# Sparse attention: scaling the probabilities one turn ahead of their transposes

## The chip, the core and the metric

The kernel runs on one core of one Trainium2 chip. The core has a matrix engine (TensorE, PE in the profile; its weight loads are the row PEld), a vector engine (DVE), a scalar engine (ACT), a general engine (GpSimd, POOL) and an engine that issues transfers (SyncE, SP). All work on a shared on-chip memory, SBUF; the matrix engine writes its results into eight PSUM banks. The metric is the device time of one execution in microseconds; a lower one is better.

## The reference

One decoder layer on 512 tokens of width 1024 in float32: a half-step feed-forward network, a token mixer, a second half-step feed-forward network, each between RMS norms. The token mixer adds native sparse attention and dilated attention. The change lies in the sparse attention, which has 8 heads of width 64 on 2 key groups and three branches:

```python
g = jax.nn.sigmoid(gates)
return g[..., 0:1] * o_cmp + g[..., 1:2] * o_slc + g[..., 2:3] * o_win
```

Each branch is a softmax over biased scores times values. With 512 tokens the selected branch takes all of its 8 blocks of 64, and the window of 512 covers everything, so both the selected and the window branch are full causal attentions, with keys and values of their own. Dividing a row of probabilities by its sum and weighting the branch by its gate are one factor to a query row, gate over sum.

## The kernel before

All products with weights run as three matmuls on high and low parts (`mm3`, lines 128 to 132), the parts made by a cast on ACT (line 107) and a subtraction on DVE (line 108). `nsa` (line 1006) does the sparse attention. It first makes keys, values, gates and the inputs of the compressed branch, then runs a loop of turns over a list of 16 entries, `heads`: 4 query tiles times 2 halves times 2 branches (0 selected, 1 window). An entry is called a head here. With `LAG = 2` there are 18 turns; turn n scores head n and finishes head n-2. In the order of the program a turn holds:

- in every fourth turn, the query projection of the next tile, and `cmp_pair` (line 909), the compressed branch of two heads;
- `hb_probs` (line 961) for head n-2: `gated` (lines 905 to 907) makes four factors, gate over sum, by three small DVE instructions; the probabilities of four query tiles are multiplied by them in place, those of tile 3 (512 columns) on ACT (line 969), those of the other three (384, 128 and 256 columns) on POOL (line 971); then ten transposes on PE (line 980) bring them into three PSUM banks, tag T, of which there are two, and each bank is split into a high and a low part (lines 107 and 108);
- `hb_scores` (line 945) for head n: for three PSUM banks of tag S, matmuls for the scores (lines 724 and 725), then for each query tile a DVE instruction that adds the position bias and takes the extreme of a row (the min-add, line 730), and an exponential on ACT that also sums the row (line 731). The results lie in three of 11 SBUF slots, tag SP;
- `hb_values` (line 992) for head n-2: eight matmuls (line 995) of the transposed probabilities with the values into a bank of tag V, and after the window branch the compressed part and `fold` (line 998);
- in the first turns the compressed branch's hidden layer, and in every third turn a filler (`merge_unit`, line 1079), a projection for a later stage.

Every instruction belongs to one engine, and the engine runs its own in a fixed order. That order is made when the program is compiled: a planner that works with its own estimates of durations goes through the instructions, gives each engine those whose inputs are ready, and takes the one that stands earlier in the program where several are. A stretch of the program can be kept in written order; `nsa` does not do that. Semaphores then make each instruction wait for its inputs.

Of the kernel before, what the change touches and what calls it, by code (L numbers as in the profile page):

```python
# [60 lines left out]
class Layer:  # L61
# [896 lines left out]
                self.softmax_rows(pt[n][:, o:o + ncol], b[:, o:o + ncol], w[:, S - ncol:S], st[:, 0, t:t + 1], st[:, 1, t:t + 1])  # L958
        return st, pt

    def hb_probs(self, st, pt, gate):

        nc = self.nc
        self.gated(st[:, 1], NT, gate)
        for t in (3, 2, 0, 1):
            n, o = self.PLACE[t]
            pp = pt[n][:, o:o + (t + 1) * P]
            if t == NT - 1:
                nc.scalar.mul(pp, pp, st[:, 1, t:t + 1])
            else:  # L970
                nc.gpsimd.tensor_scalar(pp, pp, st[:, 1, t:t + 1], None, op0=OP.mult)  # L971
        out = {}
        for kbs in ((0,), (1, 3), (2,)):
            b = self.bank("T")
            ncols = 0
            for kk in kbs:
                _, o = self.TPLACE[kk]
                for t in range(kk, NT):
                    pn, po = self.PLACE[t]
                    nc.tensor.transpose(b[:, o + (t - kk) * P:o + (t - kk + 1) * P],  # L980
                                        pt[pn][:, po + kk * P:po + (kk + 1) * P], self.ident)
                    ncols += P
            hi, lo = self.slot("PT", F32R)[:, 0:ncols], self.slot("PT", F32R)[:, 0:ncols]
            self.split(hi, lo, b[:, 0:ncols])
            for kk in kbs:
                _, o = self.TPLACE[kk]
                c = slice(o, o + (NT - kk) * P)
                out[kk] = hi[:, c], lo[:, c]
        return out
# [16 lines left out]
    def nsa(self, fillers):  # L1006
        nc = self.nc
        ident = lambda v: v
        r = self.wcols([(C_KC, 256)])
        src = [r[:, :, 0:P], r[:, :, P:2 * P]]  # L1010
        r2 = self.wcols([(C_KS, P), (C_KW, P)])
        src2 = [r2[:, :, 0:P], r2[:, :, P:2 * P]]
        early = []
        for s, tag in zip(src + src2, "FFSV"):
            w = self.wslots(s, "SP") if tag == "V" else None
            early.append(self.proj_T(s, self.bank(tag), (0, 2 * P), w))
            if len(early) in (2, 3):
                self.pending.pop(0)()
        for n, (b, w) in enumerate(early):
            self.proj_T(None, b, (2 * P, S), w)  # L1020
        rows = [self.block_rows(b) for b, _ in early[:2]]
        kw = early[3][0]
        vw = self.v_weights()
        kparts = [self.k_parts(early[2][0], ident)]
        gs = [self.blocks(0, rows[0])]
        kparts.append(self.k_parts(kw, ident))
        gs.append(self.blocks(1, rows[1]))
        self.v_nsa(vw)
        early = self.hidden_early(0)
        self.oh, self.ol = [], []  # L1030
        heads = [(i, half, br) for i in range(4) for half in range(2) for br in range(2)]
        qs, cmps, ws, live = {}, {}, {}, {}
        probs = {}
        for n in range(len(heads) + LAG):
            if n < len(heads) and n % 4 == 0:
                i = n // 4
                b, _ = self.proj_T(self.wcols([(i * 64, 64), (256 + i * 64, 64)]))
                qs[i] = self.q_parts(b, ident)
                if i:
                    cmps[i] = self.cmp_pair(i, qs[i])  # L1040
            m = n - LAG
            if m >= 0:
                i, half, br = heads[m]
                probs[m] = self.hb_probs(*live.pop(m), self.gate[:, :, (i + 4 * half) * 3 + 1 + br])
            if n < len(heads):
                i, half, br = heads[n]
                h = i + 4 * half
                if br == 0:
                    ws[h] = self.slot("W")
                    nc.vector.tensor_scalar(ws[h], self.dm, -(2.0 ** -(h + 1)), None, op0=OP.mult)  # L1050
                kb, ka = kparts[br]
                live[n] = self.hb_scores(qs[i][half], ka[half], kb, half, ws[h])
            if m >= 0:
                i, half, br = heads[m]
                if br == 0:
                    out = self.bank("V")
                    if half == 0:
                        of = self.slot("of")
                self.hb_values(probs.pop(m), br, half, out, br == 0)
                if br == 1:  # L1060
                    nc.tensor.matmul(out, self.vcs[half], cmps[i], start=False, stop=True, skip_group_check=True)
                    self.fold(of, half, out[0:64], out[64:128])
                    if half == 1:
                        hi, lo = self.slot("x", F32R), self.slot("x", F32R)
                        self.split(hi, lo, of)
                        self.oh.append(hi)
                        self.ol.append(lo)
            if n < 2:
                self.hidden(n, gs[n], early)
                if n == 0:  # L1070
                    early = self.hidden_early(1)
                else:
                    hid = self.gelu()
            if n == 2:
                self.compressed(hid)
                cmps[0] = self.cmp_pair(0, qs[0])
            fillers()
# [465 lines left out]
```

## Time and profile before

| | us |
|---|---|
| median of 3 runs | 1134.19 |
| lowest and highest run | 1133.87, 1138.51 |
| the profiled execution | 1135.51 |
| its span, first to last instruction | 1133.7 |
| PE busy in the span | 1119.2 |
| DVE busy | 907.2 |
| ACT busy | 638.1 |
| POOL busy | 76.8 |

The times are of whole executions; the profile is of one execution, and its span leaves out what lies before the first and after the last instruction. A row of a profile that groups instructions has line, engine, operation, what is written and read, shapes and count, then the busy time and the mean duration in ns, then the idle time of that engine in front of them and what ended it. A row of the timeline has start, duration, engine, line and the same names, and in brackets the idle time in front. PE's busy time is modelled at its ends: consecutive matmuls overlap, so that a short wait need not show as idle time. The loop of turns lies between 398 and 533 us.

### The profile page before, as it was taken

Reading aid. Unit: us, or ns where it says so; the run is one execution under the profiler, and the core shown is the slowest. Engines: PE = TensorE matmul, PEld = TensorE weight load, DVE = VectorE, ACT = ScalarE, POOL = GpSimd, SP = SyncE. Lnnn points to the kernel's source line nnn. Section 1 sums busy time; section 2 is a strip of 40 time slices with the busy share of each in tenths; the row PEclk is TensorE's granted clock in tenths of the full one; section 3 lists DMA queues with packets and bytes.
Section 4 is the critical chain, followed back from the end, with each engine's and each line's share of the span. In section 5 each row is a group of like instructions: output and inputs, shape, how many; then the busy total and the mean of one; then the engine's idle time right before and its main releaser. Section 6 shows DMA issues by size and latency. Waiting matters only on the chain.

```text
span 1133.7 us, 18456 instructions
## 1 busy us (share of the span) xinstructions
PE 1119.2 (99%) x6921; PEld 1001.7 (88%) x6921; DVE 907.2 (80%) x1563; ACT 638.1 (56%) x1145; POOL 76.8 (7%) x112
## 2 busy tenths in 40 slices
PE   9999999999999999999999999999999999999997
PEld 7889999998888987778888998787989999998886
DVE  6989999879676889687665687986778888979774
ACT  5435555567563788677565634645445555557562
POOL 1000000000012033343000000000000000000000
PEclk9999999999999999999999999999999999999999
DMA  9996665588763542111476758683233424357862
GB/s 320 328 305 194 182 209 173 155 273 287 266 204 96 176 131 85 54 40 56 140 251 224 253 177 292 210 290 118 66 121 122 131 86 127 124 170 239 285 224 84
DMA packets 152908, 206.01 MB, mean 182 GB/s; under 512 B 19794, under 2 KB 97906, under 8 KB 152564
## 3 DMA queue, kind: packets, MB, share of 16 engines
q1 hardware_dynamic: 152816, 204.85, 55.7%
q8 instruction: 54, 0.88, 0.3%
q14 instruction: 34, 0.28, 0.1%
q10 hardware_dynamic: 4, 0.00, 0.0%
HBM read 165.45 MB, written 39.37 MB: 181 GB/s over the span
## 4 chain that ended last, share of the span: by engine, by line
PE 89%; DVE 5%; ACT 2%; issue 1%; DMA 1%; POOL 1%; SPq 0%; POOLq 0%; DVEq 0%; ACTq 0%
PE pb_F L132 11%; PE pb_F L130 11%; PE pb_F L131 11%; PE pb_S L132 8%; PE pb_S L131 8%; PE pb_S L130 8%; PE pb_T L130 6%; PE pb_T L132 6%; PE pb_T L131 6%; PE pb_V L131 3%; PE pb_V L130 3%; PE pb_V L132 3%; PE pb_V L995 2%; PE pb_T L980 1%; DVE SP_s L730 1%
## 5 line engine op out<-in xcount | busy, mean ns | idle before, releaser
L107 ACT CAST whi<-raw 128x1024 fp32r<-128x1024 f32 (+1 forms) x215 | 219.9, 1023 | 251.9 <-issue 68.2
L108 DVE TENSOR_TENSOR wlo<-raw,whi 128x1024 fp32r<-128x1024 f32 (+1 forms) x215 | 255.0, 1188 | 94.9 <-ACT whi L107 91.3
L130 PE MATMUL pb_F<-xh_t,whi 128*128 128x512 f32 (+1 forms) x392 | 142.7, 364 | 0.4 <-ACT whi L107 0.4
L132 PE MATMUL pb_F<-xh_t,wlo 128*128 128x512 f32 (+1 forms) x392 | 141.6, 361 | 0.5 <-DVE wlo L108 0.5
L131 PE MATMUL pb_F<-xl_t,whi 128*128 128x512 f32 (+1 forms) x392 | 141.8, 362 | 0.0
L107 ACT CAST whi<-tmp_t 128x1024 fp32r<-128x1024 f32 x51 | 53.5, 1048 | 60.9 <-PE pb_S L131 22.0
L132 PEld LDWEIGHTS pb_F<-xh_t,wlo 128*128 128x128 f32 x392 | 74.1, 189 | 10.8 <-DVE wlo L108 1.0
L130 PEld LDWEIGHTS pb_F<-xh_t,whi 128*128 128x128 f32 x392 | 74.1, 189 | 10.4 <-ACT whi L107 0.6
L131 PEld LDWEIGHTS pb_F<-xl_t,whi 128*128 128x128 f32 x392 | 74.2, 189 | 9.6
L108 DVE TENSOR_TENSOR wlo<-tmp_t,whi 128x1024 fp32r<-128x1024 f32 x51 | 62.4, 1223 | 25.2 <-ACT whi L107 23.9
L130 PE MATMUL pb_S<-xh_t,whi 128*128 128x256 f32 (+1 forms) x240 | 73.2, 305 | 0.0
L132 PE MATMUL pb_S<-xh_t,wlo 128*128 128x256 f32 (+1 forms) x240 | 73.0, 304 | 0.0
L131 PE MATMUL pb_S<-xl_t,whi 128*128 128x256 f32 (+1 forms) x240 | 73.0, 304 | 0.0
L130 PE MATMUL pb_T<-xh_t,whi 128*128 128x256 f32 (+1 forms) x184 | 54.5, 296 | 0.0
L132 PE MATMUL pb_T<-xh_t,wlo 128*128 128x256 f32 (+1 forms) x184 | 54.3, 295 | 0.0
L131 PE MATMUL pb_T<-xl_t,whi 128*128 128x256 f32 (+1 forms) x184 | 54.3, 295 | 0.0
L152 POOL TENSOR_TENSOR rs_t<-rs_t,mhalf_t 128x1 f32<-128x1 f32 x24 | 17.5, 727 | 542.7 <-DVE rs_t L148 542.7
L971 POOL TENSOR_SCALAR SP_s<-SP_s,st_t 128x384 f32<-128x384 f32 (+2 forms) x48 | 45.8, 970 | 107.1 <-DVE st_t L907 77.3
L131 PEld LDWEIGHTS pb_S<-xl_t,whi 128*128 128x128 f32 x240 | 45.9, 191 | 1.9
L130 PEld LDWEIGHTS pb_S<-xh_t,whi 128*128 128x128 f32 x240 | 45.9, 191 | 1.9
L132 PEld LDWEIGHTS pb_S<-xh_t,wlo 128*128 128x128 f32 x240 | 45.9, 191 | 1.9
L108 DVE TENSOR_TENSOR PT_s<-pb_T,PT_s 128x512 fp32r<-128x512 f32 (+1 forms) x72 | 39.2, 559 | 6.3 <-ACT PT_s L107 5.6
(822 smaller groups left out, 3363.8 us busy)
## 6 DMA issues: line engine op xcount, KB each, us to landing
raw<-in_ffn_w_up_dram SPq DMA_DIRECT2D x36, 512.0 KB, 5.3
raw<-in_w_in_dram SPq DMA_DIRECT2D x18, 1024.0 KB, 5.7
raw<-in_ffn_w_gate_dram SPq DMA_DIRECT2D x35, 512.0 KB, 4.9
raw<-in_ffn_w_down_dram SPq DMA_DIRECT2D x14, 1024.0 KB, 5.7
raw<-tdram SPq DMA_DIRECT2D x14, 1024.0 KB, 5.2
NN_s<-in_ffn_w_down_dram SPq DMA_DIRECT2D x22, 512.0 KB, 5.0
tdram<-NN_s SPq DMA_DIRECT2D x22, 512.0 KB, 3.9
raw<-in_ffn_w_down_dram SPq DMA_DIRECT2D x6, 768.0 KB, 5.8
```

The lines of the kernel that those rows point to most:

```text
L107: self.last_cast = self.nc.scalar.copy(dsthi, src).ins
L108: self.last_rest = self.nc.vector.tensor_sub(dstlo, src, dsthi.bitcast(F32)).ins
L130: mm(out, lhi, rhi, start=start, stop=False, skip_group_check=skip)
L131: mm(out, lhi, rlo, start=False, stop=False, skip_group_check=skip)
L132: mm(out, llo, rhi, start=False, stop=stop, skip_group_check=skip)
L152: nc.gpsimd.tensor_tensor(out=r, in0=v, in1=self.mhalf, op=OP.pow)
L730: nc.vector.tensor_tensor_reduce(p, s, w, -1.0, FLOOR, OP.add, OP.min, st_m)
L971: nc.gpsimd.tensor_scalar(pp, pp, st[:, 1, t:t + 1], None, op0=OP.mult)
L980: nc.tensor.transpose(b[:, o + (t - kk) * P:o + (t - kk + 1) * P], pt[pn][:, po + kk * P:po + (kk + 1) * P], self.ident)
L995: self.nc.tensor.matmul(out[:, kk * P:S], v, pp, start=first and kk == 0 and pi == 0, stop=False, skip_group_check=True)
```

## The change

`hb_probs` is cut in two. `hb_scale` holds `gated` and the four multiplies, `hb_probs` the transposes and splits. In turn n, the transposes of head n-2 are emitted first, then the scaling of head n-1, then the scores of head n. So the scaling of a head stands one turn earlier in the program than its transposes, behind the transposes of the head before it and ahead of the scores of the head after it. The number and kind of instructions stays the same, and so does what each of them reads and writes.

```diff
-    def hb_probs(self, st, pt, gate):
+    def hb_scale(self, st, pt, gate):
 
         nc = self.nc
         self.gated(st[:, 1], NT, gate)
...
             else:
                 nc.gpsimd.tensor_scalar(pp, pp, st[:, 1, t:t + 1], None, op0=OP.mult)
+
+    def hb_probs(self, pt):
+
+        nc = self.nc
         out = {}
         for kbs in ((0,), (1, 3), (2,)):
             b = self.bank("T")
...
             m = n - LAG
             if m >= 0:
-                i, half, br = heads[m]
-                probs[m] = self.hb_probs(*live.pop(m), self.gate[:, :, (i + 4 * half) * 3 + 1 + br])
+                probs[m] = self.hb_probs(live.pop(m)[1])
+            if 0 <= n - 1 < len(heads):
+                i, half, br = heads[n - 1]
+                self.hb_scale(*live[n - 1], self.gate[:, :, (i + 4 * half) * 3 + 1 + br])
             if n < len(heads):
                 i, half, br = heads[n]
                 h = i + 4 * half
```

## The prediction, made before the changed kernel ran

> **What bounds the kernel now.** I read the page first, then the busy time of the attention stage by stretches, then the rows of the instructions that the change moves, then who waits for them.
>
> ```profile
> span 1133.7 us, 18456 instructions
> PE 1119.2 (99%) x6921; PEld 1001.7 (88%) x6921; DVE 907.2 (80%) x1563; ACT 638.1 (56%) x1145; POOL 76.8 (7%) x112
> ...
> PE 89%; DVE 5%; ACT 2%; issue 1%; DMA 1%; POOL 1%; SPq 0%; POOLq 0%; DVEq 0%; ACTq 0%
> ```
>
> The page says that TensorE (PE) works in 99% of the span and carries 89% of the chain that ended last; 1133.7 - 1119.2 = 14.5 us are all the idle time that it shows. A change gains only what it takes from PE's work or from PE's waits. The change touches neither a matmul nor a transpose, so only waits are left, and only those of the sparse attention, which lies between 398 and 535 us:
>
> ```profile
> core 0: us, PE busy (x) PEld busy (x) DVE busy (x) ACT busy (x) POOL busy (x), PEclk, DMA share, GB/s
> 400.00:430.00 30.00, 29.28 (x173) 24.55 (x172) 25.48 (x78) 23.78 (x61) 8.76 (x9) 1.00 0.39 98
> 430.00:460.00 30.00, 29.53 (x173) 23.71 (x172) 27.70 (x86) 25.59 (x62) 14.68 (x15) 1.00 0.25 79
> ...
> sum 135.00, PE 133.46 PEld 108.01 DVE 112.15 ACT 103.22 POOL 48.41; mean PE 26.69 PEld 21.60 DVE 22.43 ACT 20.64 POOL 9.68
> ```
>
> Of these 135 us PE is idle in 1.54, DVE in 22.85, ACT in 31.78, POOL in 86.6; the clock is full. Matmul ends are modelled and overlap, so PE's small waits hide inside its busy time; they show better at the weight loads (PEld), each of which must have its operand:
>
> ```profile
> PEld pb_V L995 <- ACT PT_s L107: 4.0, 13, 0.7
> PEld pb_T L980 <- DVE PT_s L108: 1.8, 6, 0.4
> PEld pb_S L724 <- DVE st_t L730: 1.6, 6, 0.6
> PEld pb_V L995 <- DVE PT_s L108: 1.4, 6, 0.3
> ```
>
> These are the largest such waits between 395 and 540 us (us in total, times, longest). The transposes (L980) wait for the split that empties their PSUM bank, the value matmuls (L995) for the split of the transposed probabilities. No row names the scaling, POOL's L971 or ACT's L969, as what a load on PE waited for.
>
> **The scaling is already far ahead.** In the program the scaling of head m stands in turn m+2 right in front of its transposes. The rows of the trace show another order. First POOL's own rows, then the first transposes of the same heads on PE; heads are counted in order, three POOL instructions and ten transposes to a head (0, 3, 5 and 6 in one row, 7, 14, 15):
>
> ```profile
> 409.18 2.99 POOL L971 TENSOR_SCALAR SP_s<-SP_s,st_t 128x384 f32<-128x384 f32 x3 [50.19 <-DVE st_t L907]
> ...
> 432.53 3.54 POOL L971 TENSOR_SCALAR SP_s<-SP_s,st_t 128x384 f32<-128x384 f32 x3 [8.91 <-DVE st_t L907]
> ...
> 451.20 5.78 POOL L971 TENSOR_SCALAR SP_s<-SP_s,st_t 128x384 f32<-128x384 f32 x6 [6.62 <-DVE st_t L907]
> 457.74 2.73 POOL L971 TENSOR_SCALAR SP_s<-SP_s,st_t 128x384 f32<-128x384 f32 x3 [0.76 <-PE pb_T L980]
> ...
> 517.76 2.73 POOL L971 TENSOR_SCALAR SP_s<-SP_s,st_t 128x384 f32<-128x384 f32 x3 [1.07 <-DVE st_t L907]
> 522.28 2.73 POOL L971 TENSOR_SCALAR SP_s<-SP_s,st_t 128x384 f32<-128x384 f32 x3 [1.79 <-DVE st_t L907]
> ```
>
> ```profile
> 413.90 1.03 PE L980 MATMUL pb_T<-ident_t,SP_s 128*128 128x128 f32 x8
> 431.24 0.60 PE L980 MATMUL pb_T<-ident_t,SP_s 128*128 128x128 f32 x4
> 447.33 0.60 PE L980 MATMUL pb_T<-ident_t,SP_s 128*128 128x128 f32 x4
> 477.37 0.60 PE L980 MATMUL pb_T<-ident_t,SP_s 128*128 128x128 f32 x4
> 483.70 1.06 PE L980 MATMUL pb_T<-ident_t,SP_s 128*128 128x128 f32 x8
> 524.67 0.27 PE L980 MATMUL pb_T<-ident_t,SP_s 128*128 128x128 f32 x1
> 528.57 0.27 PE L980 MATMUL pb_T<-ident_t,SP_s 128*128 128x128 f32 x1
> ```
>
> Head 0 is scaled at 412.2 and transposed from 413.9 (1.7 us later); head 3 at 436.1 and 447.3 (11.2); head 6 at 457.0 and 477.4 (20.4); head 7 at 460.5 and 483.7 (23.2); head 14 at 520.5 and 524.7 (4.2); head 15 at 525.0 and 528.6 (3.6). The second PE row is head 1, whose transposes belong to turn 3; the scaling of head 3, which the program puts into turn 5, begins on POOL 1.3 us after them. So the compiled order does not follow the program's: an engine is given what is ready, and the place in the program only ranks what is ready at once. The scaling needs nothing but the exponentials of its head, so it already runs about where the change writes it. That is the ground of my forecast: the edit changes a rank, not a dependence.
>
> **The change part by part.** Sixteen times, the three small DVE instructions of gated, one ACT multiply and three POOL multiplies are emitted ahead of the scores of the next head and not ahead of the own transposes. Nothing is removed or added, no DMA belongs to the step, and SP's queue is not passed; PSUM banks and SBUF slots are asked for in the same order. The prices of what moves:
>
> ```profile
> L969 ACT ACTIVATE SP_s<-SP_s,st_t 128x512 f32<-128x512 f32 x16 | 11.6, 724 | 1.3 <-DVE st_t L907 1.2
> L905 DVE TENSOR_SCALAR st_t<-st_t 128x4 f32<-128x4 f32 x16 | 3.0, 188 | 0.4 <-ACT SP_s L731 0.4
> L906 DVE RECIPROCAL st_t<-st_t 128x4 f32<-128x4 f32 x16 | 2.7, 169 | 0.2
> L907 DVE TENSOR_TENSOR st_t<-st_t,gate_t 128x4 f32<-128x4 f32 x16 | 2.6, 162 | 0.2
> ```
>
> *The work itself* is 0.519 us of DVE for a head (8.3 in all), 0.72 of ACT (11.6) and 2.73 to 3.54 of POOL: the same before and after, 0.
>
> *What comes earlier.* The most that a scaling can move is to the end of its head's exponentials. Head 14 shows the delay now, on ACT the read of the last sum, on DVE the first and last step of gated:
>
> ```profile
> 514.50 0.19 ACT L731 ACTIVATION_READ_ACCUMULATOR SP_s<-SP_s,st_t 128x1 f32 x1
> 514.83 0.27 DVE L905 TENSOR_SCALAR st_t<-st_t 128x4 f32<-128x4 f32 x1
> 517.43 0.16 DVE L907 TENSOR_TENSOR st_t<-st_t,gate_t 128x4 f32<-128x4 f32 x1
> ```
>
> The sum is known at 514.69, gated ends at 517.59, and 0.52 of that is work: 2.4 us could go, because other DVE work stood between its steps. The transposes of that head had 4.2 us to spare already, and none of those above had less than 1.7, so an earlier scaling takes nothing from a wait: gain 0. Bounds: nothing, or at the best all of the split and bank waits above if the whole rhythm of transposes shifted with it (4.0 + 1.8 + 1.4 = 7.2 us). I take 0, since POOL is in none of these rows.
>
> *What comes later.* The three DVE steps now rank ahead of the next head's min-adds (L730), which free the score banks that PE's L724 fills. Their cover is DVE's idle 22.85 us, against 8.3. If that cover were gone, PE would pay 8.3, five times the 1.6 us that L724 waits for min-adds now. ACT's multiply ranks ahead of the next head's exponentials in the same way, 11.6 against 31.78 idle; exponentials free no bank, so behind them stands only the next scaling. POOL's three pass only the zeroing of key tiles and two index fills for the next stage, with 86.6 us idle. I take 0 again; bounds 0 and 8.3.
>
> [...]
>
> **The sum.** The profiled execution took 1135.51 us (span 1133.7 and 1.8 around it), 1.3 over the median of the runs. 1135.5 + 0 - 0 + 0 = 1135.5 there, and 1134.2 against the median 1134.19. I forecast 1134.2, with an own range of 1131 to 1138 for the new ranks' accidents, about the size of half of either bound.
>
> **The rivals.** *The rhythm of the transposes improves.* With the scaling ranked higher, the planner may place the transposes a little earlier, with more PE work between a transpose and its value matmuls, and the waits for splits vanish. For it: heads 5, 14 and 15 have only 3 to 4 us to spare, which a planner with its own times may see as none. Against it: heads 6 and 7 had over 20 us and were not taken sooner. Price 7.2 us: 1127.0.
>
> *DVE stands in its order (slower).* An instruction is fixed in its engine's order when the program is compiled. If gated is placed close behind the exponentials, DVE reaches it before ACT has read the last sum, and stands with the next head's min-adds and the splits behind it. The gap from the last min-add to the last sum is what DVE would stand:
>
> ```profile
> 401.45 0.08 DVE L730 DVE_READ_ACCUMULATOR2_ANT st_t<- 128x1 f32 x1
> ...
> 513.86 0.08 DVE L730 DVE_READ_ACCUMULATOR2_ANT st_t<- 128x1 f32 x1
> ```
>
> ```profile
> 402.64 0.19 ACT L731 ACTIVATION_READ_ACCUMULATOR SP_s<-SP_s,st_t 128x1 f32 x1
> ```
>
> That is 402.83 - 401.53 = 1.3 us in head 0 and 514.69 - 513.94 = 0.75 in head 14. With the 0.52 of work it makes 1.27 to 1.82 for a head; from 22.85 / 16 = 1.43 on, DVE has no idle time left and PE waits. At 1.82 the excess is 16 x 0.39 = 6.3 us, on top of the 1.6 that L724 waits now growing likewise to about twice: 1134.2 + 6.3 + 1.6 = 1142. For it: DVE is at 83% here and 27.7 of 30 in its fullest stretch. Against it: gated runs close behind the exponentials already, and its row shows only 0.4 us idle ended by ACT. [...]
>
> *The change does not do what it says.* If all ranks fall out alike, every engine's order is the same and the time is 1134.2 within the 0.3 us between the two lower runs shown.
>
> **How the numbers follow.** A measurement of this kernel can tell about 0.5%, 5.7 us, from no change. Forecast 0.58; identical order 0.11; better rhythm 0.15; DVE standing 0.16. The forecast's own range and the identical order lie within 0.5%: 0.69 for no change. The better rhythm at 1127.0 is faster by 0.63%: 0.15. DVE standing at 1142 is slower by 0.7%: 0.16. The range 1127 to 1141 holds the forecast and about half of each rival, some 0.84.
>
> **What would show it.** Right: the POOL scalings end several us ahead of the first transposes as now, gated's three steps follow each other more closely, PE's idle time between 400 and 535 us stays near 1.5 us and the loads of L980 and L995 keep their 7 us of waits. The better rhythm would show in fewer waits of L995 for ACT's PT_s. DVE standing would show as idle time of DVE ahead of L905 ended by ACT's L731, above 10 us where it is 0.4, and as more waits of L724 for L730. What would make the forecast wrong altogether is another order of PE's work far from the scaling, fillers and projections falling elsewhere, so that the later stages meet other loads.

## The result, and the profile after

The changed kernel takes 1141.49 us in the median of six runs (1140.68 to 1142.44), the kernel before 1134.74 in six runs beside it (1133.87 to 1138.51). The ratio is 1.0057, with a 95% interval of 1.0046 to 1.0068: 0.57% slower, some 6.5 us. The ratio is estimated from all runs and not from the two medians. The profiled execution took 1140.68 us with a span of 1138.9.

The page of the changed kernel, its first lines and the chain by engine:

```profile
span 1138.9 us, 18462 instructions
...
PE 1118.7 (98%) x6921; PEld 1001.4 (88%) x6921; DVE 906.1 (80%) x1563; ACT 637.6 (56%) x1145; POOL 79.6 (7%) x112
...
PE 87%; DVE 5%; ACT 4%; issue 2%; POOL 1%; DMA 1%; SPq 0%; POOLq 0%; DVEq 0%; ACTq 0%
```

The work is the same to 0.5 us on PE; what has grown is PE's idle time, from 14.5 to 20.2 us. The stretches of the attention stage, with the columns of the prediction (stretch; its length; busy time of PE, PEld, DVE, ACT, POOL with counts; granted clock; DMA share; GB/s):

```profile
400.00:430.00 30.00, 25.94 (x146) 21.56 (x144) 20.42 (x55) 19.48 (x49) 10.68 (x9) 0.94 0.40 97
430.00:460.00 30.00, 28.97 (x165) 23.72 (x165) 25.97 (x92) 23.44 (x61) 9.38 (x10) 1.00 0.25 80
...
sum 135.00, PE 127.98 PEld 103.56 DVE 107.20 ACT 100.06 POOL 50.95; mean PE 25.60 PEld 20.71 DVE 21.44 ACT 20.01 POOL 10.19
```

PE's idle time in these 135 us has gone from 1.54 to 7.02, and 4.06 of that lie in the first 30 us, where the granted clock is 0.94. The waits of PE and of its weight loads in the stage (us in total, times, longest) name what came in:

```profile
PEld pb_V L999 <- ACT PT_s L107: 7.3, 19, 0.9
PEld pb_T L984 <- POOL SP_s L971: 4.4, 2, 2.8
...
PE pb_T L984 <- POOL SP_s L971: 3.8, 2, 2.6
```

L984 are the transposes (L980 before), L999 the value matmuls (L995 before). Twice a transpose waited for POOL's scaling, which no row of the kernel before shows. The timeline gives the place, head 0; first PE, with the idle time in front in brackets:

```profile
404.01 0.40 PE L725 MATMUL pb_S<-KB_s,Q_s 128*128 128x512 f32 x1
405.58 0.33 PE L984 MATMUL pb_T<-ident_t,SP_s 128*128 128x128 f32 x1 [1.17 <-POOL SP_s L971]
408.55 0.48 PE L984 MATMUL pb_T<-ident_t,SP_s 128*128 128x128 f32 x1 [2.64 <-POOL SP_s L971]
408.68 0.78 PE L130 MATMUL pb_F<-xh_t,whi 128*128 128x512 f32 x1
...
413.44 0.39 PE L130 MATMUL pb_F<-xh_t,whi 128*128 128x512 f32 x1
```

and POOL's and DVE's rows beside it:

```profile
403.69 4.80 POOL L971 TENSOR_SCALAR SP_s<-SP_s,st_t 128x384 f32<-128x384 f32 x3 [46.02 <-DVE st_t L907]
...
405.29 2.35 DVE L108 TENSOR_TENSOR wlo<-raw,whi 128x1024 fp32r<-128x1024 f32 x2
407.56 0.35 DVE L905 TENSOR_SCALAR st_t<-st_t 128x4 f32<-128x4 f32 x1
```

Before, head 0 was scaled from 409.18 to 412.2 and transposed from 413.90. Now it is scaled from 403.69 to 408.49, so that the scaling begins 5.5 us earlier and ends 3.7 earlier. But its first two transposes stand from 405.58 on, 8.3 us earlier, in the middle of the scaling, and PE, which keeps its order, stands for it twice, 1.17 and 2.64 us. Everything behind them on PE, the hidden layer and the projections, needs no scaling and waits all the same. The matmul L130 at 408.68 lasts 0.78 us, the same one at 413.44 0.39: the granted clock is at half, 0.50. The stretches in which it changes:

```profile
404.72:408.13 3.41, 0.33 (x1) 0.14 (x1) 3.41 (x9) 2.54 (x9) 3.41 (x3) 1.00 0.57 112
408.13:411.55 3.42, 3.00 (x12) 2.81 (x13) 0.12 (x1) 0.00 (x0) 0.37 (x1) 0.50 1.05 325
```

Counting PE's matmuls in order of their start, from 0 on, shows how much of the loss lies here. Number 2550 starts at 388.1 us before and 1.3 us earlier after (the clock came up 3.05 us earlier at the start of that execution); number 2700 starts at 414.8 and 4.0 us later; at 553.7 (number 3450) the lag is 5.1 us, and so it is at the end. So 5.3 us are lost between 388 and 415, and 1.1 us in the rest of the stage. The step of 5.3 is the 3.8 us of waiting and, by an estimate, half of the 3.41 us at half clock, 1.7, together 5.5.

### The profile page after: what moved, and what is told of

It reads as the page before. It is cut to its first block, busy times and chain, and to the rows that moved or that the text cites. A ratio compares the mean times of both kernels' runs of the same rounds, so it can differ in the third digit from the quotient of the medians.

```text
span 1138.9 us, 18462 instructions
## 1 busy us (share of the span) xinstructions
PE 1118.7 (98%) x6921; PEld 1001.4 (88%) x6921; DVE 906.1 (80%) x1563; ACT 637.6 (56%) x1145; POOL 79.6 (7%) x112
## 4 chain that ended last, share of the span: by engine, by line
PE 87%; DVE 5%; ACT 4%; issue 2%; POOL 1%; DMA 1%; SPq 0%; POOLq 0%; DVEq 0%; ACTq 0%
PE pb_F L130 10%; PE pb_F L132 10%; PE pb_F L131 10%; PE pb_S L131 8%; PE pb_S L130 8%; PE pb_S L132 8%; PE pb_T L130 6%; PE pb_T L132 6%; PE pb_T L131 6%; PE pb_V L131 3%; PE pb_V L130 3%; PE pb_V L132 3%; PE pb_V L999 1%; PE pb_T L984 1%; DVE SP_s L730 1%
## 5 line engine op out<-in xcount | busy, mean ns | idle before, releaser
L130 PE MATMUL pb_F<-xh_t,whi 128*128 128x512 f32 (+1 forms) x392 | 142.5, 364 | 0.8 <-DVE Q_s L1211 0.4
L130 PEld LDWEIGHTS pb_F<-xh_t,whi 128*128 128x128 f32 x392 | 74.4, 190 | 10.7 <-ACT whi L107 0.6
L130 PE MATMUL pb_S<-xh_t,whi 128*128 128x256 f32 (+1 forms) x240 | 73.2, 305 | 0.0
L971 POOL TENSOR_SCALAR SP_s<-SP_s,st_t 128x384 f32<-128x384 f32 (+2 forms) x48 | 48.3, 1020 | 112.4 <-DVE st_t L907 81.3
L130 PE MATMUL pb_T<-xh_t,whi 128*128 128x256 f32 (+1 forms) x184 | 53.9, 293 | 0.0
L130 PEld LDWEIGHTS pb_S<-xh_t,whi 128*128 128x128 f32 x240 | 45.9, 191 | 1.9
```

The source lines that it names most:

```text
L130: mm(out, lhi, rhi, start=start, stop=False, skip_group_check=skip)
```

## The experiments

Two theories. A: one place. The planner puts head 0's transposes where the chip isn't ready for them; the wait and the clock that falls behind it are the loss. B: the new rank costs a little in each of the 16 turns, DVE standing for exponentials, as the slower rival of the prediction had it. The first four kernels share 27 runs of the kernel before, median 1135.02 us (1133.68 to 1136.38). Their diffs are against the changed kernel.

### Head 0 scaled late, all others early

```diff
+            if m == 0:
+                i, half, br = heads[0]
+                self.hb_scale(*live[0], self.gate[:, :, (i + 4 * half) * 3 + 1 + br])
             if m >= 0:
                 probs[m] = self.hb_probs(live.pop(m)[1])
-            if 0 <= n - 1 < len(heads):
+            if 1 <= n - 1 < len(heads):
```

> The changed kernel, but head 0 is scaled where it was before, in turn 2 right in front of its transposes; heads 1 to 15 are scaled one turn ahead. Theory A (one place: the planner puts head 0's first transposes on PE at 405.6 us, before POOL has scaled the rows; PE stands 1.17 + 2.64 us and its clock is halved for 3.41 us, which costs 1.7 more): the step of some 5.3 us between 388 and 415 us is gone, about 1.1 us remain, so 1136 us; no wait of L984 for POOL above 0.5 us, clock full. Theory B (the new rank costs in every turn, DVE standing for the exponentials): nearly all stays, 1140 us.

Measured: 1134.59 us (1134.22 to 1137.48, 11 runs), ratio 1.0001, interval 0.9992 to 1.0009. Counted by matmuls, the step between 388 and 415 us is 0.03 us; 0.55 more come by 553.7, and 0.2 behind that. The first stretch of this kernel and its first transposes:

```profile
400.00:430.00 30.00, 29.55 (x177) 25.00 (x176) 25.55 (x79) 23.48 (x61) 9.22 (x9) 1.00 0.39 98
```

```profile
414.48 1.03 PE L984 MATMUL pb_T<-ident_t,SP_s 128*128 128x128 f32 x8
```

PE's idle time is back to 0.45 us and the transposes to 414.48. Fifteen of the sixteen new ranks cost nothing that can be measured, and bring nothing. They also move little: by the traces of this kernel and the kernel before, the scaling of thirteen of these heads begins within 1 us of where it began, that of head 13 1.4 us earlier and that of head 5 2.9. B falls. A had left 1.1 us and said 1136.

### Head 0 alone scaled early

```diff
+            if m > 0:
+                i, half, br = heads[m]
+                self.hb_scale(*live[m], self.gate[:, :, (i + 4 * half) * 3 + 1 + br])
             if m >= 0:
                 probs[m] = self.hb_probs(live.pop(m)[1])
-            if 0 <= n - 1 < len(heads):
+            if n == 1:
```

> The kernel before, but head 0 alone is scaled one turn ahead; heads 1 to 15 stand right in front of their transposes. Theory A: the whole step of some 5.3 us is there, 1140 us, with L984 waiting for POOL 3 us or more and a half clock for about 3 us. Theory B: one turn of sixteen, so within 0.5 us of the kernel before, 1135 us.

Measured: 1140.48 us (1139.61 to 1141.68, 5 runs), ratio 1.0048, interval 1.0036 to 1.0061. One sixteenth of the change makes nearly the whole loss, some 5.5 of the 6.5 us. PE's two waits for POOL are the same, 1.17 and 2.64 us. The clock in this kernel's profile was at half for two stretches on end, 6.83 us, where I had expected about 3:

```profile
403.39:406.80 3.41, 1.48 (x7) 0.65 (x5) 3.41 (x12) 3.41 (x8) 2.85 (x3) 1.00 0.19 41
406.80:410.21 3.41, 1.40 (x5) 1.21 (x6) 1.71 (x3) 0.72 (x4) 1.96 (x1) 0.50 1.01 268
410.21:413.63 3.42, 3.42 (x18) 3.42 (x18) 0.00 (x0) 0.41 (x1) 0.00 (x0) 0.50 0.47 159
```

Here the wait fell across the border of two stretches, both little used, and each was followed by one at half clock.

### All ranks changed, head 0's transposes held back on PE

```diff
...
-                    nc.tensor.transpose(b[:, o + (t - kk) * P:o + (t - kk + 1) * P],
-                                        pt[pn][:, po + kk * P:po + (kk + 1) * P], self.ident)
+                    with self.tc.issue_after(self.last_hid) if first else nullcontext():
+                        nc.tensor.transpose(b[:, o + (t - kk) * P:o + (t - kk + 1) * P],
+                                            pt[pn][:, po + kk * P:po + (kk + 1) * P], self.ident)
...
```

`last_hid`, set at L814, is the last matmul of the second hidden layer; `first` is true for head 0 alone.

> The changed kernel in every rank, but head 0's ten transposes are held on PE behind the last matmul of the second hidden layer (L814), where they stood in the kernel before. Theory A: the scaling may stay early, only the place of the transposes costs: 1136 us, no half clock. Theory B: 1140 us, since no rank of the scaling is changed.

Measured: 1136.24 us (1135.17 to 1138.76, 11 runs), ratio 1.0015, interval 1.0006 to 1.0024. The scaling keeps its early rank, and some 5 of the 6.5 us are gone. PE now does the hidden layer first and reaches the transposes 1.7 us later than in the changed kernel. They still stand 6.6 us ahead of the 413.90 of the kernel before. What is left has its own row, a shorter wait of the same kind:

```profile
407.31 0.27 PE L985 MATMUL pb_T<-ident_t,SP_s 128*128 128x128 f32 x1
408.21 0.44 PE L985 MATMUL pb_T<-ident_t,SP_s 128*128 128x128 f32 x2 [0.63 <-POOL SP_s L971]
```

So most of the cost lies not in the early scaling itself, but in the place that the transposes get by it.

### One of the three multiplies taken from POOL

```diff
...
-            if t == NT - 1:
+            if t == NT - 1 or first and t == 1:
                 nc.scalar.mul(pp, pp, st[:, 1, t:t + 1])
...
```

Here too `first` is true for head 0 alone.

> The changed kernel, but of head 0 the multiply of query tile 1 (256 columns) runs on ACT and not on POOL. In the changed kernel that one POOL instruction took 3.00 us where such take 0.92, while DVE ran two subtractions with both inputs in SBUF, and PE's second transpose stood 2.64 us for it. Theory A with contention: that wait goes, the first of 1.2 us may stay, the idle time falls under 2 us and the clock is not halved: 5.3 - 2.6 - 1.7 = 1 us of the step is left, 1137 us. If the clock falls on any idle time of PE, 1138.5. Theory B: 1140 us.

Measured: 1136.05 us (1135.58 to 1138.09, 11 runs), ratio 1.0011, interval 1.0002 to 1.0019. The planner moved the second transpose behind two projections and twelve hidden matmuls, so that this kernel differs in its order too; the first still stands 1.16 us for POOL, the long wait is gone:

```profile
405.69 0.34 PE L984 MATMUL pb_T<-ident_t,SP_s 128*128 128x128 f32 x1 [1.16 <-POOL SP_s L971]
```

The profiled execution was this kernel's longest, 1138.09, and it had a half clock, although PE had waited only 1.16 us. Two more executions of the same kernel show whether that belongs to the kernel:

> The same kernel as e5_third_scale_on_act, one more execution with its profile. If the clock is judged over fixed stretches of 3.413 us whose phase differs between executions, the wait of L984 for POOL is 1.16 us again, and the half clock of 3.41 us is there in some executions and not in others; one without it is about 1.7 us shorter between 388 and 415 us than the 2.65 us step of the first.

> As for the execution before this one: the same wait, and the half clock there or not by the phase alone.

They took 1135.11 and 1135.61 us, with a kernel before of 1133.91 beside them. The same stretches in the first execution and in the first of the two others:

```profile
402.47:405.88 3.41, 2.05 (x12) 1.21 (x11) 3.41 (x13) 3.41 (x6) 1.84 (x2) 1.00 0.03 7
405.88:409.30 3.42, 3.42 (x16) 3.23 (x16) 2.46 (x5) 1.90 (x8) 0.00 (x0) 0.50 0.87 194
```

```profile
403.03:406.44 3.41, 2.24 (x13) 1.71 (x14) 3.41 (x9) 3.41 (x9) 1.83 (x2) 1.00 0.31 69
406.44:409.86 3.42, 3.42 (x25) 3.16 (x25) 2.13 (x6) 2.15 (x9) 0.00 (x0) 1.00 0.95 251
```

In both the transposes wait 2.8 us for POOL in all, PE and weight loads together, and only the borders of the stretches lie elsewhere. Counted by matmuls the step between 388 and 415 us is 2.65 us with the half clock, 1.17 and 1.11 without. So this half stretch cost about 1.5 us of its 3.41, near the 1.7 that I took.

### POOL's multiply beside DVE, by itself

In the changed kernel POOL's third multiply of head 0 (256 columns) is the longest of all 48, while its like mostly take 0.92 us:

```profile
L971 POOL TENSOR_SCALAR SP_s<-SP_s,st_t x48: 597/922/2996, 403.7 to 528.3; 128x384 f32<-128x384 f32 x16, 128x128 f32<-128x128 f32 x16, 128x256 f32<-128x256 f32 x16
```

It ran beside the two subtractions of DVE at 405.29. A small kernel puts the two side by side:

```python
for _ in range(8):
    nc.gpsimd.tensor_scalar(s, s, st, None, op0=OP.mult)   # 128 x 256, in each of four parts
...
for _ in range(8):
    nc.vector.tensor_sub(z, x, y)                          # second part: 128 x 1024, all in SBUF
...
for _ in range(12):
    nc.vector.tensor_sub(z[:, 0:S], pb, y[:, 0:S])         # third part: one input in PSUM
```

> A small kernel that computes nothing of the layer: POOL multiplies 128 x 256 rows by a factor four times eight times, alone; while DVE subtracts two tiles of 128 x 1024 that both lie in SBUF, eight times; while DVE subtracts with one input in PSUM, twelve times of 128 x 512; and alone again. If the 3.00 us of the changed kernel's scaling came from DVE's two SBUF inputs, a POOL multiply takes 0.92 us alone and beside the PSUM form, and stands for whole subtractions of 1.2 us beside the SBUF form, over 2 us in the mean or alternating with them. If it came from any work of DVE, the PSUM form slows it as much; if from something else in that place (the transfers, ACT), none of the four parts differs.

POOL's four parts of eight multiplies, in order:

```profile
5.79 8.03 POOL L37 TENSOR_SCALAR s<-s,st 128x256 f32<-128x256 f32 x8 [5.37 <-DVE z L45]
14.38 11.78 POOL L37 TENSOR_SCALAR s<-s,st 128x256 f32<-128x256 f32 x8 [0.56 <-DVE st L42]
26.71 8.03 POOL L37 TENSOR_SCALAR s<-s,st 128x256 f32<-128x256 f32 x8 [0.55 <-DVE st L42]
35.67 8.33 POOL L37 TENSOR_SCALAR s<-s,st 128x256 f32<-128x256 f32 x8 [0.93 <-DVE st L42]
```

Beside the PSUM form eight multiplies take the 8.03 us that they take alone; beside the SBUF form 11.78. So it isn't any work of DVE that delays POOL: what differs is where DVE's inputs lie. The two forms differ in width too (512 columns and 1024), but twelve of the PSUM form on end delay nothing. The fourth part was meant to be alone and takes 0.3 us more, all in its first multiply (1.22 us), beside which DVE copies one SBUF tile to another for 0.69 us. So some work of DVE with a single input in SBUF delays POOL as well. The size failed: one multiply took 1.32 us here (the first 1.88), not over 2. All these subtractions write one tile, and each starts only after the one ahead has ended (eight of 1.36 us in 11.13); in the changed kernel the second starts 0.07 us before the first ends. So once more with four tiles to write to:

```diff
-        nc.vector.tensor_sub(z, x, y)
+        nc.vector.tensor_sub(zs[i % 4], x, y)
```

> The small kernel again, but DVE's subtractions write four tiles in turn, so that one starts before the one ahead of it has ended, as the two subtractions beside the scaling in the changed kernel do (406.43 before 406.50). If POOL gets in only where DVE leaves a gap, one multiply of POOL stands for the whole series of SBUF subtractions, 8 x 1.14 = 9 us, and the other seven follow alone at 0.92; then 3.00 us is two subtractions waited out. If they alternate as before at 1.32 us for a multiply, the gap is not the reason and the size of the 3.00 us stays open.

```profile
14.31 14.40 POOL L38 TENSOR_SCALAR s<-s,st 128x256 f32<-128x256 f32 x8 [0.56 <-DVE st L43]
```

```profile
L38 POOL TENSOR_SCALAR s<-s,st x32: 922/922/2931, 5.7 to 45.3; 128x256 f32<-128x256 f32 x32
```

The multiplies beside the subtractions took 2.93, 2.38, 2.38 and 2.38 us, the other four 0.92. Neither of my two cases: POOL doesn't stand for the whole series. Four multiplies were delayed beside eight subtractions (1.22 us in the median), so by these numbers it got in after two of them. But 2.93 is nearly the 3.00 of the changed kernel, with only DVE beside it. Why two and not one isn't settled. By an estimate from these rows, without the delay the scaling would have ended 2.08 us sooner (3.00 - 0.92), and PE's second wait would have been about 0.6 us of its 2.64.

## Why the prediction was wrong

**The forecast of no change failed: 1134.2 us was forecast, 1141.49 measured, 0.5 us above the range.** By the prediction's own steps:

- *What bounds the kernel* held: PE's work stayed, only its waits changed.
- *The scaling is already far ahead* held for heads 1 to 15. Their new ranks cost nothing, ratio 1.0001 without head 0's move, and shifted most of these scalings by less than 1 us. The edit changed a rank and no dependence, as argued.
- *What comes earlier: gain 0, because no transposes had less than 1.7 us to spare.* This is the step that failed. It took the transposes to stay where they were while the scaling moved. But a transpose too gets its place in PE's order from the planner, by the planner's own idea of when its input is ready. With the scaling ranked earlier, the first of head 0's transposes stood 8.3 us further ahead, while the scaling began only 5.5 us sooner on the chip and ended 3.7 sooner. That the planner took them for ready there is inferred from that order; its own times are not on record, nor why it moved this head's transposes and not the others'. The 1.7 us to spare, the smallest in the list and of all sixteen heads, turned into two waits, 3.8 us, where the bounds of that step, 0 to 7.2 us of gain, had only a gain.
- *What comes later: 0 of a possible 8.3 us* held. L724 waits for min-adds 0.8 us, where it waited 1.6:

```profile
PEld pb_S L724 <- DVE st_t L730: 0.8, 4, 0.2
```

- *The work itself: the same before and after, 0* failed on POOL at one place. Head 0's three multiplies took 4.80 us, where the prediction counted on 2.73 to 3.54 for a head. One of them took 3.00 where its like mostly take 0.92, 2.08 us more, beside two subtractions of DVE with both inputs in SBUF; with the spare time gone it counted. That two on end delay POOL so is from the second small kernel, where it took 2.93.
- *The slower rival* forecast 1142 and was nearly the time, by luck, since its cause did not occur. Its mechanism is of the right kind, an instruction fixed in its engine's order ahead of what it needs (here PE's transposes, 1.17 and 2.64 us), and it was looked for on the wrong engine. Its sign was to be over 10 us of DVE idle ahead of L905; the row has 1.3:

```profile
L905 DVE TENSOR_SCALAR st_t<-st_t 128x4 f32<-128x4 f32 x16 | 2.9, 182 | 1.3 <-ACT SP_s L731 1.3
```

- *The clock* had no term in the sum at all: "the clock is full" was read as a given. It fell to 0.50 behind the stretch of PE's wait, in which PE was busy for 0.33 of 3.41 us, and by the estimate and the counts above added some 1.5 to 1.7 us to 3.8.
- The last sentence of the prediction, on another order of PE's work with fillers and projections falling elsewhere, came nearest to what happened. But it looked far from the scaling, where the new order lay right at it, and it gave this no price and no place among the chances.

The remaining 1.1 us of the changed kernel, after 415 us, were not taken apart; the kernel without head 0's move shows about half of that and no measurable difference.

## What to carry to other kernels

When a producer is moved up in a program that a planner orders, its consumer can move too, here that of one head in sixteen; ask for each consumer where the planner could now put it and which work, needing nothing of it, would then stand behind it. Slack in a trace is slack for that order only, and the smallest one in the list (here 1.7 us, head 0) is where to look first. If the early producer is wanted, hold the consumer on its engine behind the work that it must not block; here that took back most of the loss and brought no gain (1136.24 us).

## What the runs showed of the hardware

**Within an execution the granted clock changed after whole multiples of 3.413 us.** In the changed kernel it was full from 12.19 to 408.13 us, 395.946 us or 116 times 3.4133, and then half for one such stretch, 3.413 us; with head 0 alone early for two, 6.827. In the kernel before it was full for 1116.158 us, 327 such stretches. In one execution of the kernel with a third multiply on ACT it was half behind a stretch with a wait of 1.16 us and 2.05 us of PE busy; behind a stretch with 2.24 it stayed full in the next. In all eight traces of the layer's kernels together, and leaving out the end of an execution, where PE has no work left, the clock fell to half behind three stretches, in which PE was busy for 0.33, 1.48 and 2.05 us. The least busy stretch behind which it stayed full lies in the kernel with the order held, with 2.17 (2.18 in the changed kernel, 2.19 in the kernel before):

```profile
348.50:351.92 3.42, 2.17 (x18) 2.12 (x18) 2.98 (x8) 2.14 (x6) 0.77 (x5) 1.00 0.40 144
```

By PE's busy time, whose ends are modelled, the border lies between 2.05 and 2.17 us in these traces; what exactly is counted isn't shown.

**In the second small kernel a POOL multiply on SBUF took up to 2.93 us, where it takes 0.92 alone, beside DVE's subtractions with both inputs in SBUF.** There each subtraction starts before the one ahead of it has ended (eight of 1.29 us in 9.77); where each waits for the one ahead, in the first small kernel, the multiply took 1.32. DVE pays less: its subtraction took 1.21 us at the least, and 1.36 in the mean beside POOL in the first small kernel. DVE subtractions that read PSUM delayed nothing here: eight multiplies took 8.03 us beside twelve of them, 0.69 us each, and 8.03 alone. A DVE copy within SBUF of 0.69 us delayed the multiply beside it to 1.22.
